# Two z tiles move from the attention's fill to a pair of seven block products between the gates

## The chip, the core and the metric

One Trainium2 chip, one NeuronCore. TensorE (PE) does matmuls and transposes into PSUM, VectorE (DVE), ScalarE (ACT) and GpSimd (POOL) do the elementwise work, and SyncE (SP) issues nearly all DMAs from one queue, in order. The metric is the device time of one execution in microseconds. The kernel before takes 902.21 us, the median of three runs from 901.38 to 902.74.

## The reference, cut to what matters

```python
h = rms_norm(x, g_pre[l], NORM_EPS)
proj = jnp.einsum('bsd,dn->bsn', h, w_in[l])
qa, ka, va, fa, za, qb, kb, vb, zb, gates = jnp.split(proj, SPLIT_POINTS, axis=-1)
...
ya = merge_heads(ya) * jax.nn.silu(za)
...
yb = merge_heads(yb) * jax.nn.silu(zb)
gate_a, gate_b = jnp.split(jax.nn.sigmoid(gates), N_BRANCHES, axis=-1)
merged = (gate_a * jnp.einsum('bsw,wd->bsd', ya, w_branch[l, 0])
          + gate_b * jnp.einsum('bsw,wd->bsd', yb, w_branch[l, 1]))
y = jnp.einsum('bsd,de->bse', merged, w_out[l])
x = x + rms_norm(y, g_post[l], NORM_EPS)
```

Sequence 1024, model width 1024. `za` and `zb` are 512 columns each of the same projection as everything else; together they are eight z tiles of 128 columns, kept transposed (128 columns x 1024 positions, float32). They aren't needed until the two attentions are done and their outputs are multiplied by silu(z).

## The kernel before, in words

Every float32 product is made of three matmuls of a rounded part and its remainder: with left operand `hi + lo` and right operand `h0 + h1`, hi h0, hi h1 and lo h0 (`project`, L328 on). A projected tile takes 2 chunks of 512 positions x 8 blocks of 128 along the model width x 3 = 48 matmuls of 128 x 128 on 128 x 512.

The kernel goes through these stages:

1. Norm, transposition of h into `hT` and the v projections.
2. Attention, eight units `u` in a loop: 0 to 3 are the heads of the differential attention, 4 to 7 pairs of heads of the forgetting attention. A unit is cut into groups of two score rows (L492 and L493: scores; L495: DVE takes the minimum that the softmax needs; L501: ACT's exponential; then a scaling on POOL or ACT). The group before has its probabilities transposed on PE (L522), split into parts on ACT and DVE (L525, L526), and multiplied with v (L546).
3. Between groups, the loop calls functions from a list `fill`: the four projection chunks (q and k) of the unit after, then the z tiles that `ZFILL[u]` names, then the sums of squares that `SFILL[u]` names. The count called after each group goes with the share of the unit's weight that is done. A z tile (`z_tasks`, by `spill_tasks`) loads 512 KB of weights, splits them on POOL and DVE, makes 48 matmuls into two accumulators, copies each out on ACT (L433) and stores it to the scratch tensor `z_d[t]` (L434). `ZFILL` gives z tiles 0, 1, none, 2, 3, 4, 5 and (6, 7) to the units 0 to 7. In unit 7, the last task of the list and the `gl` gate's two chunks are cut into pieces by hand (`LATE`, and the lists at the end of the stage).
4. Gates: 16 gate tiles, d = 0 to 7 and two branches. d = 0 is made plainly; d = 1 to 7 are made as pairs (`gates_pair`): the two branches' tiles of one d are one 256 x 1024 matrix, split in 2 x 2 blocks against `hT` in 2 x 2 blocks, and multiplied by seven block products in the place of eight (`wino`, with the combinations of the left side made in `left_operands` and those of the right side, `t_d`, made in stage 1 and loaded in `h_load`). Each block product is 4 x 3 = 12 matmuls (L818), so that a pair takes 84 where plainly it takes 96. A pair needs four combinations on POOL (L780), seven splits (L767 on ACT, L768 on DVE, for two of them on POOL), one copy on ACT (L821), seven sums on DVE (L811), four sigmoids (L880) and four stores (L881).
5. After each pair the attention outputs that `YORD[d]` names are loaded and multiplied by silu(z) (`y_load`, `y_work`; z is read back at L870). `y_work(t, c)` reads `z_d[(t + 4) % 8]`, so z6 is read at d = 5 and z7 at d = 6.
6. The branch products (L978), the merge and the output projection with its own seven products (L818, tiles `x_o`).

The raw weights of a pair are loaded by `gate_raw` (L902) into the two buffers `wraw`; the two loads of the next pair wait until the four combinations and the splits of the one before have read them.

The order of the instructions on each engine isn't the program's alone: when the kernel is built, a planner with costs of its own draws up each engine's order, with the program's order as priority, and takes later instructions forward where earlier ones would wait. `tc.issue_after(i)` keeps what it encloses behind `i`. The order is fixed then; on the chip, engines wait for each other by semaphores.

Of the kernel before, what the change touches and what calls it, by code (L numbers as in the profile page):

```python
# [16 lines left out]
P = 128  # L17
S = 1024
D = 1024
KT = D // P  # L20
NB = S // P
CH = 512
# [11 lines left out]
GFILL = 5  # L34
LATE = ((), ((0, 0, 3),), ((0, 3, 6),), ((0, 6, 8), (1, 0, 2)), ((1, 2, 5),), ())
TAIL = 2
ZFILL = ((0,), (1,), (), (2,), (3,), (4,), (5,), (6, 7))
BIG = 3.0e38
EPS = 1e-6
SUB_EPS = 1e-5  # L40
# [2 lines left out]
QA, KA_, VA, ZA, QB, KB_, VB, ZB, GT = 0, 512, 1024, 1544, 2056, 2568, 3080, 3592, 4104  # L43
# [7 lines left out]
def tile_hybrid_block(  # L51
# [18 lines left out]
    nc = tc.nc  # L70
# [17 lines left out]
        out=trim, in_=trim, pattern=[[-1, P]], base=0, channel_multiplier=1,  # L88
# [25 lines left out]
    z_d = [dram.tile([P, S], F32, name=f"z_d{t}") for t in range(8)]  # L114
# [196 lines left out]
    def load_w(name, src, hi_act=False, lo_pool=False, pieces=None, behind=(None, None)):  # L311
        raw = wpool.tile([P, KT, P], F32, tag="wraw", name=f"raw_{name}")
        for ks, piece in pieces or [(slice(0, KT), src)]:
            nc.sync.dma_start(raw[:, ks], piece)
        hi = wpool.tile([P, KT, P], F32R, tag="whi", name=f"hi_{name}")
        lo = wpool.tile([P, KT, P], F32R, tag="wlo", name=f"lo_{name}")
        with tc.issue_after(behind[0]) if behind[0] else ExitStack():
            if hi_act:
                nc.scalar.copy(hi, raw)
            else:  # L320
                nc.gpsimd.tensor_scalar(hi, raw, 1.0, 1.0, op0=ALU.mult, op1=ALU.mult)
        with tc.issue_after(behind[1]) if behind[1] else ExitStack():
            eng = nc.gpsimd if lo_pool else nc.vector
            eng.tensor_tensor(lo, raw, hi, op=ALU.subtract)
        return hi, lo

    def w_cols(c0):
        return w[:, c0:c0 + P].rearrange("(k p) n -> p k n", p=P)  # L328

# [10 lines left out]
    with ExitStack() as st:  # L340
# [73 lines left out]
            return T, tasks  # L414

        def z_tasks(t):
            return spill_tasks(f"z{t}", (ZA + t * P) if t < 4 else (ZB + (t - 4) * P), z_d[t])

        def spill_tasks(nm, c0, dst):
            box = {}  # L420

            def mk(c):
                def run(ks=range(KT)):
                    if not box:
                        box[0] = load_w(nm, w_cols(c0))
                    if ks[0] == 0:
                        box["ps"] = pj.tile([P, CH], F32, tag="pj", name=f"p{nm}_{c}")
                    ps = box["ps"]
                    lasts[0] = project(ps, box[0], c, ks)
                    if ks[-1] < KT - 1:  # L430
                        return
                    zs = stg.tile([P, CH], F32, tag="raw", name=f"s{nm}_{c}", bufs=4)
                    nc.scalar.copy(zs, ps)  # L433
                    nc.sync.dma_start(dst[:, c * CH:(c + 1) * CH], zs)  # L434
                return run
            return [mk(0), mk(1)]
# [251 lines left out]
        for u in range(8):  # L688
# [8 lines left out]
            if u + 1 < 8:  # L697
                T, tasks = unit_proj(u + 1)
                fill += tasks
            for t in ZFILL[u]:  # L700
                fill += z_tasks(t)
# [70 lines left out]
    def left_operands(nm, a11, a12, a21, a22):  # L772

        comb = {}

        def combine(name, x, y, op):
            if name not in comb:
                comb[name] = wx.tile([P, 4, P], F32, tag="comb", name=f"{name}_{nm}", bufs=4)
                eng = nc.vector if nm in ("o0", "o1") and name in ("S1", "S2") else nc.gpsimd
                eng.tensor_tensor(comb[name], x, y, op=op)  # L780
            return comb[name]

        def s1():
            return combine("S1", a21, a22, ALU.add)

        def s2():
            return combine("S2", s1(), a11, ALU.subtract)

        def get(m):
            v = {1: lambda: a11, 2: lambda: a12, 4: lambda: a22, 5: s1, 6: s2,  # L790
                 3: lambda: combine("S4", a12, s2(), ALU.subtract),
                 7: lambda: combine("S3", a11, a21, ALU.subtract)}[m]()
            pool, tag = ((wpool, "whi"), (wpool, "wlo"), (wx, "wop"))[opn[0] % 3]
            opn[0] += 1
            t = pool.tile([P, 2, 4, P], F32R, tag=tag, name=f"a{m}_{nm}")
            split(t, v, nc.gpsimd if m in (2, 4) and nm not in ("o2", "o3") else nc.vector)
            return t
        return get
# [68 lines left out]
    def y_work(t, c):  # L867
        ys = yz[t // 2][:, t % 2, c * CH:(c + 1) * CH]
        zs = tmp.tile([P, CH], F32, tag="t", name=f"zs{t}_{c}")
        nc.sync.dma_start(zs, z_d[(t + 4) % 8][:, c * CH:(c + 1) * CH])  # L870
        if t < 4:
            rb = tmp.tile([P, CH], F32, tag="t", name=f"rb{t}_{c}")
            nc.sync.dma_start(rb, rs_d[t:t + 1, c * CH:(c + 1) * CH].to_broadcast([P, CH]))
            nc.vector.scalar_tensor_tensor(ys, ys, gsub, rb, op0=ALU.mult, op1=ALU.mult)
        nc.vector.tensor_tensor(ys, ys, zs, op=ALU.mult)
        nc.scalar.activation(zs, zs, AF.Sigmoid)
        nc.vector.tensor_tensor(ys, ys, zs, op=ALU.mult)

    def gate_out(d, br, c, g, src):
        nc.scalar.activation(g, src, AF.Sigmoid)  # L880
        nc.sync.dma_start(g_d[d][br][:, c * CH:(c + 1) * CH], g)  # L881
# [13 lines left out]

    raws, lastraw = {}, [None]

    def gate_raw(d):
        raws[d] = []
        for br in range(2):  # L900
            r = wpool.tile([P, KT, P], F32, tag="wraw", name=f"raw{d}_{br}")
            lastraw[0] = nc.sync.dma_start(r, w_cols(GT + br * D + d * P)).ins  # L902
            raws[d].append(r)

    def h_load():
# [7 lines left out]
                gate_raw(1)  # L913
            h_ops[m] = [[t[:, k, :] for k in range(4)] for t in ts[m]]

    def gates_pair(d, order):
        raw = raws[d]
        left = left_operands(f"g{d}", raw[0][:, 0:4], raw[0][:, 4:8], raw[1][:, 0:4], raw[1][:, 4:8])
        run_all(wino(f"g{d}", left, h_ops, order,
                     *(lambda t, br=br, c=c: gate_out(d, br, c, t, t)  # L920
                       for br in range(2) for c in range(2))))

    ORD = (1, 6, 5, 7, 2, 3, 4)
    GATE = (1, 2, 4, 6, 5, 7, 3)
# [4 lines left out]
    for d in range(1, KT):  # L929
        if d not in raws:  # L930
            gate_raw(d)
        with tc.issue_after(lastraw[0]):
            for t, c in YORD[d]:
                if c == 0:
                    y_load(t)
        gates_pair(d, (1, 2, 3, 4, 6, 5, 7) if d == 1 else GATE if d < KT - 1 else (7, 5, 6, 4, 1, 2, 3))
        if d == 2:
            for c in range(2):
                g = tmp.tile([P, CH], F32, tag="t", name=f"g0_0_{c}")
                nc.sync.dma_start(g, gl_d[:, c * CH:(c + 1) * CH])  # L940
                gate_out(0, 0, c, g, g)
        for t, c in YORD[d]:
            y_work(t, c)
    tst.close()


# [58 lines left out]
    r = {}  # L1005
# [172 lines left out]
```

## Time and profile before

| | us |
|---|---|
| median of three runs | 902.21 (901.38 to 902.74) |
| the profiled execution | 901.03 |
| its span in the profile | 899.3 |
| first projection of attention (start of k, unit 0) | 108.1 |
| plain gate of d = 0 | 582.2 to 593.2 |
| seven pairs of gates | 593.2 to 727.8 |
| branch products | 727.8 to 814.9 |

The profile is of one execution on the one core, and the granted clock of TensorE was 0.998 in it. Busy times are unions of the intervals of an engine's instructions; the matmuls' ends are modelled and overlap the next one's start, so what a matmul costs is read from the distance of starts.

### The profile page before, as it was taken

To read this page: it belongs to the slowest core of one execution; us is meant where nothing else is said; L and a number is where in the kernel's file an instruction comes from. 1 tells how busy PE (TensorE), PEld (TensorE's weight loads), DVE (VectorE), ACT (ScalarE), POOL (GpSimd) and SP (SyncE) were. 2 spreads that over 40 slices of the span, in tenths; PEclk is the share of its full clock that TensorE was granted. 3 is DMA by queue.
4 is the path that set the end of the run, shared out by engine and by line. 5 is a ranking of instruction groups with operands and counts; after the bars stand their busy time and mean duration, and the time that the engine had idled before them with its cause. 6 is when DMAs were issued, how large, how long until landed. Compare 5 with 4: busy or idle time off the path is not lost.

```text
span 899.3 us, 13795 instructions
## 1 busy us (share of the span) xinstructions
PE 882.4 (98%) x4600; PEld 745.4 (83%) x4600; DVE 581.8 (65%) x1122; ACT 430.4 (48%) x865; POOL 406.0 (45%) x398
## 2 busy tenths in 40 slices
PE   8999999999999999999999999999999999999996
PEld 5999987788888878888888888888888888888885
DVE  6766555767666744456647556627766896648896
ACT  7523224665756653364545646724543362314352
POOL 2134224735646535254344435516534323483961
PEclk9999999999999999999999999999999999999999
DMA  8566656756557763645636430397766598210495
GB/s 303 191 241 249 221 160 166 176 139 170 154 136 188 183 172 80 184 98 133 188 94 158 137 105 26 85 410 243 240 200 203 185 359 299 80 39 1 124 194 173
DMA packets 138185, 154.79 MB, mean 172 GB/s; under 512 B 12145, under 2 KB 98161, under 8 KB 137090
## 3 DMA queue, kind: packets, MB, share of 16 engines
q1 hardware_dynamic: 133744, 151.55, 56.2%
q0 software_dynamic: 4224, 2.10, 2.0%
q8 instruction: 36, 0.59, 0.3%
q14 instruction: 35, 0.29, 0.1%
q10 hardware_dynamic: 146, 0.27, 0.1%
HBM read 86.17 MB, written 38.34 MB: 138 GB/s over the span
## 4 chain that ended last, share of the span: by engine, by line
PE 84%; DMA 4%; DVE 3%; ACT 3%; SPq 2%; issue 2%; POOL 2%; POOLq 0%; DVEq 0%; ACTq 0%
PE x_g L818 15%; PE pb L978 10%; PE pv L214 10%; PE pz L334 9%; PE x_o L818 9%; PE pk L334 7%; PE pq L334 6%; PE ypf L546 4%; PE ptf L522 3%; PE ypd L546 2%; PE Sf L492 2%; PE Sf L493 2%; PE pg L334 1%; SPq L366 1%; PE pgl L334 1%
## 5 line engine op out<-in xcount | busy, mean ns | idle before, releaser
L214 PE MATMUL pv<-wvhi,hT 128*128 128x264 f32 (+2 forms) x384 | 88.1, 323 | 1.0 <-ACT wvhi L160 1.0
L334 PE MATMUL pq<-hT,hi_q 128*128 128x512 f32 x256 | 82.1, 395 | 0.0
L334 PE MATMUL pz<-hT,hi_z 128*128 128x512 f32 x256 | 81.7, 394 | 0.3 <-DVE rotq L368 0.2
L334 PE MATMUL pk<-hT,hi_k 128*128 128x512 f32 x256 | 81.7, 393 | 0.0
L978 PE MATMUL pb<-yT,hi_br 128*128 128x512 f32 x256 | 78.8, 389 | 0.0
L818 PE MATMUL x_g<-T,a_g 128*128 128x512 f32 x336 | 78.0, 391 | 0.0
L818 PE MATMUL x_o<-wo_op,a_o 128*128 128x512 f32 x336 | 77.6, 392 | 0.0
L818 PEld LDWEIGHTS x_o<-wo_op,a_o 128*128 128x128 f32 x336 | 63.0, 188 | 14.4 <-DVE a_o L768 0.5
L818 PEld LDWEIGHTS x_g<-T,a_g 128*128 128x128 f32 x336 | 63.1, 188 | 13.8
L214 PEld LDWEIGHTS pv<-wvhi,hT 128*128 128x128 f32 x384 | 64.1, 190 | 7.2 <-ACT wvhi L160 1.7
L526 DVE TENSOR_TENSOR plf<-ptf,phf 128x512 fp32r<-128x512 f32 (+1 forms) x80 | 50.1, 635 | 25.8 <-ACT phf L525 25.1
L501 ACT ACTIVATE Pd<-Pd,mxd 128x128 f32<-128x128 f32 (+7 forms) x64 | 49.8, 778 | 33.6 <-DVE mxd L495 33.5
L618 POOL TENSOR_TENSOR cb<-cb,trim 128x128 f32<-128x128 f32 x64 | 29.3, 462 | 72.0 <-DVE mxf L495 49.9
L214 PE MATMUL pv<-wvlo,hT 128*128 128x256 f32 (+2 forms) x192 | 61.7, 326 | 0.0
L501 ACT ACTIVATE Pf<-Pf,mxf 128x1024 f32<-128x1024 f32 (+3 forms) x64 | 49.7, 777 | 24.4 <-DVE mxf L495 24.1
L818 PE MATMUL x_g<-hT,a_g 128*128 128x512 f32 x252 | 59.1, 392 | 0.0
L623 POOL TENSOR_SCALAR Pf<-Pf,lf 128x1024 f32<-128x1024 f32 (+3 forms) x64 | 47.9, 753 | 21.9 <-DVE lf L622 18.3
L525 ACT CAST phf<-ptf 128x512 fp32r<-128x512 f32 (+1 forms) x80 | 42.6, 543 | 30.7 <-PE ptf L522 26.5
L978 PEld LDWEIGHTS pb<-yT,hi_br 128*128 128x128 f32 x256 | 48.0, 188 | 10.1
L818 PEld LDWEIGHTS x_g<-hT,a_g 128*128 128x128 f32 x252 | 47.3, 188 | 10.4
L334 PEld LDWEIGHTS pz<-hT,hi_z 128*128 128x128 f32 x256 | 47.3, 188 | 9.4 <-DVE rotq L368 0.5
L334 PEld LDWEIGHTS pq<-hT,hi_q 128*128 128x128 f32 x256 | 47.2, 188 | 8.9
(262 smaller groups left out, 2282.1 us busy)
## 6 DMA issues: line engine op xcount, KB each, us to landing
t_d<-t SPq DMA_DIRECT2D x16, 512.0 KB, 4.1
T<-t_d SPq DMA_DIRECT2D x8, 1024.0 KB, 8.3
raw<-in_w_in_dram SPq DMA_DIRECT2D x14, 512.0 KB, 4.8
vb_d<-vbs SPq DMA_DIRECT2D x8, 512.0 KB
va_d<-vas SPq DMA_DIRECT2D x8, 512.0 KB, 3.3
raw_k<-in_w_in_dram SPq DMA_DIRECT2D x8, 512.0 KB, 4.5
raw_q<-in_w_in_dram SPq DMA_DIRECT2D x8, 512.0 KB, 4.7
V<-vb_d SPq DMA_DIRECT2D x4, 1024.0 KB, 6.3
```

What stands on the lines that cost most here:

```text
L214: nc.tensor.matmul(ps[n], lhsT=hT[hp][k // 4][i // 4][:, k % 4, hs], rhs=wt[k][:, a:b], start=first, stop=(k == KT - 1 and hp == 1))
L334: mm = nc.tensor.matmul(ps, lhsT=a[:, k, :], rhs=hT[h][k // 4][c][:, k % 4, :], start=(k == 0 and a is hi and h == 0), stop=(k == KT - 1 a ...
L492: nc.tensor.matmul(ps, lhsT=A[:, qs], rhs=B[:, a:b], start=True, stop=False)
L501: held[0] = nc.scalar.activation(pr[:, 0:n], pr[:, 0:n], AF.Exp, bias=mx[:, len(pcs) - 1:len(pcs)], scale=-1.0, accum_out=le).ins
L522: lasts[0] = nc.tensor.transpose(pt[:, o * P:(o + 1) * P], rows[2 * g + r][:, j * P:(j + 1) * P], ident).ins
L525: nc.scalar.copy(ph[:, 0:n], pt[:, 0:n])
L526: nc.vector.tensor_tensor(pl[:, 0:n], pt[:, 0:n], ph[:, 0:n], op=ALU.subtract)
L546: lasts[0] = nc.tensor.matmul(o, lhsT=a, rhs=b[:, src], start=(j == 0 and n == 0), stop=(odd == 1 and jj == g and n == len(prods) - 1)).ins
L618: nc.gpsimd.tensor_tensor(diag, diag, trim, op=ALU.add)
L623: held[1] = nc.gpsimd.tensor_scalar(p1[:, 0:n], p1[:, 0:n], l1, 1.0, op0=ALU.mult, op1=ALU.mult).ins
L818: nc.tensor.matmul(x[m], lhsT=a[:, ai, k, :], rhs=right[m][bi][k], start=(k == 0 and n == 0), stop=(k == 3 and n == 2))
L978: nc.tensor.matmul(ps, lhsT=a[:, kk, :], rhs=yT[g][h][:, k % 2, sl], start=(k == 0 and a is hi and h == 0), stop=(k == 3 and a is lo))
```

## The change

z tiles 6 and 7 no longer are fill of attention. `ZFILL` is dealt out anew: units 4 and 6 have no z tile, units 5 and 7 have tiles 3 and (4, 5). After the pair of d = 3 and its y work, `z_pair(6)` loads the weight columns of z6 and z7 in the place of two branches' gate columns, makes the seven products with the same right operands, and stores the four results to `z_d[6]` and `z_d[7]` without a sigmoid. `gate_raw` takes the columns as an argument, and `gates_pair` what is done with each result.

```diff
-ZFILL = ((0,), (1,), (), (2,), (3,), (4,), (5,), (6, 7))
+ZFILL = ((0,), (1,), (), (2,), (), (3,), (), (4, 5))
+ZPAIR = {3: (6,)}
...
+    def z_col(t):
+        return (ZA + t * P) if t < 4 else (ZB + (t - 4) * P)
...
-    def gate_raw(d):
+    def gate_raw(d, cols=None):
         raws[d] = []
         for br in range(2):
             r = wpool.tile([P, KT, P], F32, tag="wraw", name=f"raw{d}_{br}")
-            lastraw[0] = nc.sync.dma_start(r, w_cols(GT + br * D + d * P)).ins
+            c0 = cols[br] if cols else GT + br * D + d * P
+            lastraw[0] = nc.sync.dma_start(r, w_cols(c0)).ins
             raws[d].append(r)
...
-    def gates_pair(d, order):
+    def gates_pair(d, order, out=None):
         raw = raws[d]
+        out = out or (lambda br, c, t: gate_out(d, br, c, t, t))
         left = left_operands(f"g{d}", raw[0][:, 0:4], raw[0][:, 4:8], raw[1][:, 0:4], raw[1][:, 4:8])
         run_all(wino(f"g{d}", left, h_ops, order,
-                     *(lambda t, br=br, c=c: gate_out(d, br, c, t, t)
-                       for br in range(2) for c in range(2))))
+                     *(lambda t, br=br, c=c: out(br, c, t) for br in range(2) for c in range(2))))
+
+    def z_pair(t):
+
+        def out(br, c, v):
+            nc.sync.dma_start(z_d[t + br][:, c * CH:(c + 1) * CH], v)
+
+        gate_raw(f"z{t}", [z_col(t + br) for br in range(2)])
+        gates_pair(f"z{t}", GATE, out)
...
         for t, c in YORD[d]:
             y_work(t, c)
+        for t in ZPAIR.get(d, ()):
+            z_pair(t)
     tst.close()
```

More of the change, by code (lines that the diff above doesn't have):

```diff
@@ L416, in z_tasks @@
         def z_tasks(t):
-            return spill_tasks(f"z{t}", (ZA + t * P) if t < 4 else (ZB + (t - 4) * P), z_d[t])
+            return spill_tasks(f"z{t}", z_col(t), z_d[t])
         def spill_tasks(nm, c0, dst):
```

## The prediction

> **What bounds the kernel now.** I read the page first, its busy times and the waits of the matrix engine, then the chain of work in order of time, then stretches of the attention and of the gates.
>
> ```profile
> span 899.3 us, 13795 instructions
> PE 882.4 (98%) x4600; PEld 745.4 (83%) x4600; DVE 581.8 (65%) x1122; ACT 430.4 (48%) x865; POOL 406.0 (45%) x398
> PE 84%; DMA 4%; DVE 3%; ACT 3%; SPq 2%; issue 2%; POOL 2%; POOLq 0%; DVEq 0%; ACTq 0%
> L334 PE MATMUL pz<-hT,hi_z 128*128 128x512 f32 x256 | 81.7, 394 | 0.3 <-DVE rotq L368 0.2
> L818 PE MATMUL x_g<-hT,a_g 128*128 128x512 f32 x252 | 59.1, 392 | 0.0
> ```
>
> PE is busy 98% of the span and carries 84% of the chain that ended last, so PE work that goes is worth its time, if the rest keeps up. But 392 to 394 ns is the drawn length of one 512-column matmul, and matmuls overlap. What one is worth is its spacing, which the chain in order of time shows (start, length, engine, count):
>
> ```profile
> 315.99 7.79 PE pz L334 x34
> 582.20 10.95 PE pg L334 x48
> 593.15 134.67 PE x_g L818 x588
> ```
>
> 7.79 / 34 = 0.229 us for a z matmul, 10.95 / 48 = 0.228 for a plain gate, 134.67 / 588 = 0.229 for a product of the gates' pairs: the same price in every place. The last row also says that the seven pairs (7 x 84 = 588 matmuls) run without a break.
>
> Next, how full the engines are where work is taken out and where it is put. Columns: stretch, length, busy time of PE, PEld, DVE, ACT and POOL, granted clock, DMA share, GB/s.
>
> ```profile
> 234.00:281.00 47.00, 47.00 (x264) 40.69 (x264) 32.75 (x82) 29.86 (x64) 27.92 (x23) 1.00 0.54 135
> 331.00:389.00 58.00, 57.02 (x316) 48.40 (x315) 28.81 (x78) 30.08 (x61) 27.86 (x32) 1.00 0.51 130
> 446.00:505.00 59.00, 58.71 (x335) 50.59 (x334) 35.37 (x97) 31.50 (x72) 26.25 (x40) 1.00 0.58 154
> 364.00:379.00 15.00, 15.00 (x85) 13.06 (x84) 6.76 (x17) 4.99 (x11) 2.99 (x5) 1.00 0.68 190
> 380.00:389.00 9.00, 8.02 (x56) 6.64 (x55) 7.48 (x24) 7.76 (x18) 5.94 (x10) 1.00 0.53 134
> 441.00:449.00 8.00, 8.00 (x59) 7.42 (x58) 7.88 (x21) 7.00 (x15) 4.79 (x7) 1.00 0.54 144
> 481.00:500.00 19.00, 19.00 (x109) 16.53 (x108) 13.06 (x34) 9.92 (x21) 7.71 (x10) 1.00 0.65 186
> 500.00:508.00 8.00, 7.48 (x48) 6.00 (x47) 5.88 (x16) 7.25 (x15) 4.16 (x5) 1.00 0.50 129
> 651.00:670.00 19.00, 19.00 (x85) 15.60 (x84) 12.02 (x17) 7.77 (x15) 8.89 (x6) 1.00 0.59 182
> ```
>
> The first row is about unit 2, the one attention unit that has no z tile today. The second and third are about units 4 and 6, the two that lose theirs; their z matmuls lie in 364 to 379 and 481 to 500. The rows 380:389, 441:449 and 500:508 are the short stretches that follow the z tiles of units 4, 5 and 6, in which PE has almost nothing but scores, transposes and value products. The last row is one pair of the gates, with PE full and DVE at 12.02 of 19.
>
> **The change, part by part.**
>
> *Removed: 96 matmuls of attention* (two tiles, 2 chunks x 8 k x 3). 96 x 0.229 = 22.0 us of PE. With them go, from attention, two weight splits on POOL and DVE and four copies on ACT:
>
> ```profile
> L321 POOL TENSOR_SCALAR hi_z<-raw_z x8: 1051/1056/1065, 153.1 to 498.3; 128x1024 fp32r<-128x1024 f32 x8
> L324 DVE TENSOR_TENSOR lo_z<-raw_z,hi_z x8: 1212/1226/2042, 154.2 to 499.5; 128x1024 fp32r<-128x1024 f32 x8
> raw_z<-in_w_in_dram SPq DMA_DIRECT2D x8, 512.0 KB, 4.9
> z_d<-sz SPq DMA_DIRECT2D x16, 256.0 KB, 4.3
> ```
>
> POOL 2 x 1.06 and DVE 2 x 1.23 us leave attention; none of it is on the path, so it counts nothing by itself. SP loses two loads of 512 KB and four stores there.
>
> *Added: one pair of seven products*, 7 x 12 = 84 matmuls, 84 x 0.229 = 19.2 us of PE, between the pairs of d = 3 and d = 4. So PE as a whole saves 12 x 0.229 = **2.75 us**. What the pair needs beside PE:
>
> ```profile
> L780 POOL TENSOR_TENSOR S_g<-raw x7: 1284/1290/1298, 579.4 to 697.1; 128x512 f32<-128x512 f32 x7
> L768 POOL TENSOR_TENSOR a_g<-raw,a_g x14: 1290/1526/1779, 585.0 to 714.8; 128x512 fp32r<-128x512 f32 x14
> L768 DVE TENSOR_TENSOR a_g<-S_g,a_g x28: 676/693/1784, 584.5 to 720.7; 128x512 fp32r<-128x512 f32 x28
> L811 DVE TENSOR_TENSOR c_g<-x_g,cu_g x14: 675/685/692, 609.7 to 739.1; 128x512 f32<-128x512 f32 x14
> L767 ACT CAST a_g<-raw x21: 602/617/626, 581.2 to 714.2; 128x512 fp32r<-128x512 f32 x21
> ```
>
> POOL: four combinations and two splits, at most 6 x 1.8 = 10.7 us. DVE: five splits and seven sums, 5 x 0.69 + 7 x 0.69 = 8.3 us. ACT: seven casts and a copy, 8 x 0.62 = 4.9 us, no sigmoid. All of it lies beside 19.2 us of PE and is less than a gate pair with its y work has today (12.02 us of DVE in 19). I cost it at nothing; if that cover were gone, DVE would need 19.2 us, and it has 8.3.
>
> *Moved DMAs.* The pair's two loads take both buffers of the raw weights, behind those of d = 3, and the loads of d = 4 go behind the pair's:
>
> ```profile
> raw<-in_w_in_dram SPq DMA_DIRECT2D x14, 512.0 KB, 4.8
> 630.50 0.38 SPq L902 DMA_DIRECT2D raw<-in_w_in_dram  x1
> 634.01 0.54 SPq L902 DMA_DIRECT2D raw<-in_w_in_dram  x1
> SPq L881 <- ACT cp_g L880: 40.7, 6, 9.9
> ```
>
> Pairs begin every 84 x 0.229 = 19.2 us from 593.2, so the loads issued at 630.5 and 634.0 are for the pair at 650.9: landed 4.8 us later they are 12 us early. The z pair is fed in the same way. SP also gets four stores more, which wait for DVE sums and not for ACT. Today SP stands up to 9.9 us behind one gate store, and no product is late for it; behind the z stores are the y loads and the raw loads of d = 4, which have the same 12 us. Cost 0; at the worst one landing late, 4.8 us. The z rows stored here are read by the y work of d = 5 and d = 6, after a whole pair more.
>
> *Cover taken from attention.* This is the term that the trace doesn't show. Within 364 to 379, z fills 48 x 0.229 = 11.0 of 15 us, so 4 us of attention products are covered; within 481 to 500 it is 8 of 19. These 12 us join the stretches without fill. There PE idles 0.98 of 9, 0 of 8 and 0.52 of 8 us: 1.50 in 25, or 6%. 12 x 6% = 0.7 us. Bounds: from below, nothing, since unit 2 with its projections alone keeps PE at 47.00 of 47 while DVE has 32.75; unit 6 without z would come to the same load, (35.37 - 1.23) / 48 = 71% against 32.75 / 47 = 70%. A little below nothing isn't excluded, since POOL, ACT and the projections' accumulators get freer. From above, DVE's work of the two stretches, worked out under the second rival, 4.1 us. I take 0.7: those stretches are the same products in the same units.
>
> By the Trainium skill, "TensorE: Matmul & The Clock Gate", section "Back-to-back issue gap", a lone warm matmul of 512 columns takes about 216 ns, and a stream of weight load and matmul about 131 ns. By these the saving would be 2.59 or 1.57 us; the trace disagrees with the smaller one and has 229 ns in three places.
>
> *The sum.* 22.0 - 19.2 = 2.75 saved, 0.7 given back: -2.0 us. The profiled execution took 901.03 us, 899.3 of span and 1.7 around it; it goes to 899.0. The median of the runs shown, 902.21, is 1.2 above that execution, and the same difference gives **900.2 us**. The bound of 0.2%, about what a measurement of this kernel can tell from no change, is 1.8 us, so the forecast lies only just beyond it.
>
> **The rivals.**
>
> *The saving is eaten (same).* The cover lost costs 0.95 to 4.55 us in place of 0.7. For it: PE's order is fixed beforehand by a planner with costs of its own, so a score or a transpose whose input is late on the chip holds up what is ordered behind it. Its price at the middle is 2.75: **902.2**. That the seven products save nothing, because the pair waits 2.75 us somewhere, gives the same time; 0 idle among 588 products speaks against it.
>
> *VectorE bounds the ends of units 4 and 6 (slower).* Take the z matmuls out of 481 to 508: PE has 19.00 + 7.48 - 11.0 = 15.5 us left, DVE 13.06 + 5.88 = 18.9. In 364 to 389 (without the microsecond at 379) PE has 15.00 + 8.02 - 11.0 = 12.0 left, DVE 6.76 + 7.48 = 14.2. DVE exceeds PE by 3.4 and 2.2 us, of which PE idles 0.5 and 1.0 already: 2.9 + 1.2 = 4.1 us of new waiting where DVE runs without a gap, the upper bound used above. It runs with gaps: 7.48 of 9 us, 83%, in 380 to 389. At that share DVE's 33.1 us take 39.9, 6.8 more: 4.1 + 6.8 - 2.75 = 8.2 us slower, **910.4**. It decides once the new waiting passes 4.55 us. Against it: this needs the planner to leave the stretches without projections, and matmuls of projections can be drawn into them; unit 2 lives on projections alone, and over all of unit 6 DVE has just 71%.
>
> The Trainium skill, "Perfetto Trace Analysis", section "Optimization Strategy", says that where the busiest engine changes from stage to stage, interleaving the stages can help. That speaks against this change, which takes PE-only work out of a mixed stage and gives it to one where PE alone is full; by that rule the second rival comes in. The trace agrees in part: DVE has 7.88 of 8 us in 441:449, yet PE idles none there.
>
> **How the numbers follow.** Forecast, most of the saving stays (loss under 0.95 us): 0.48. Eaten: 0.40. Slower: 0.12. So faster by over 0.2% 0.48, within 0.40, slower 0.12. The range reaches from 899.0 (no loss, 899.5, and half a microsecond of relief) to 904.0, the edge of the slower case: 0.08 below and 0.12 above are left out. The likeliest case's own range is 899.0 to 900.4.
>
> **What would show it.** PE: 4588 matmuls, with 672 in the pairs, one chain of about 672 x 0.229 = 154 us without a break. Attention from the first projection to the plain gate shorter by 21 to 22 us. Idle PE behind the projections of units 4 and 6 under 2.5 us in all, with DVE or ACT as releaser. Wrong if PE waits at L492, L522 or L546 grow by over 2 us, if the chain of pairs breaks at the z pair or behind it, or if idle comes back in unit 7.

## The result, and the profile after

The changed kernel takes 910.5 us (median of 6 runs, 907.14 to 911.59), the kernel before in the same session 901.8 (6 runs, 899.18 to 902.77). The ratio is 1.0097, with an interval of 1.0074 to 1.012. So the change makes the kernel slower by about 1%, where 0.2% faster was forecast. The profiled execution took 910.36 us.

The line numbers of the changed kernel are 4 higher in the attention and the gates: scores L496, DVE's minimum L499, exponential L505, transposes L526, value products L550. The page of the kernel after, its span, busy times and chain:

```profile
span 908.6 us, 13814 instructions
PE 886.1 (98%) x4588; PEld 745.0 (82%) x4588; DVE 586.0 (64%) x1132; ACT 433.3 (48%) x869; POOL 412.2 (45%) x402
PE 83%; DMA 4%; DVE 4%; ACT 3%; POOL 2%; issue 2%; SPq 2%; POOLq 0%; DVEq 0%; ACTq 0%
```

PE has its 12 matmuls less, and by this page it is as full as before, 98%. Nothing here shows the 9 us. Shares of the whole span hide a loss that lies in a few stretches, and a matmul at half the clock counts as busy for longer.

The chain of the kernel after in order of time (start, length, engine, count) shows the gates, with the z pair as `x_gz`, and one link of attention:

```profile
473.36 5.68 DMA sq<-y_d
...
583.28 57.72 PE x_g L822 x252
641.00 19.22 PE x_gz L822 x84
660.22 76.94 PE x_g L822 x336
```

The pairs run without a break, 57.72 + 19.22 + 76.94 = 153.88 us for 672 matmuls, against 134.67 for 588. So the added pair costs its 19.2 us and nothing more.

Then the length of attention, from the first k projection (`pk`) to the first plain gate matmul (`pg`), by the rows of these two tiles (count, then shortest, mean and longest in ns, then first and last start). Before:

```profile
L334 PE MATMUL pk<-hT,hi_k x256: 387/389/500, 108.1 to 470.7; 128*128 128x512 f32 x128
L334 PE MATMUL pg<-hT,hi_g x32: 389/389/445, 582.0 to 592.5; 128*128 128x512 f32 x32
```

After:

```profile
L338 PE MATMUL pk<-hT,hi_k x256: 387/390/498, 107.6 to 460.7; 128*128 128x512 f32 x128
L338 PE MATMUL pg<-hT,hi_g x32: 388/390/499, 572.1 to 582.7; 128*128 128x512 f32 x32
```

Attention took 582.0 - 108.1 = 473.9 us and takes 572.1 - 107.6 = 464.5. It lost 22.0 us of matmuls and got only 9.4 shorter: **12.6 us went**. (The whole span adds up: attention 9.4 shorter, its start 0.5 earlier, the pair 19.2 longer, and 908.6 - 899.3 = 9.3.) The last k projection, the one that unit 6 makes for unit 7, parts the loss roughly. Up to it 362.6 became 353.1, 9.5 of the first tile's 11.0 us. From it to the plain gate 111.3 became 111.4: of the second tile's 11.0 us nothing is kept. That tile's place was the end of unit 6.

There, the waits of 172 us of the kernel before (370 to 542: engine, tile and line, what was waited for, us in total, times, longest):

```profile
PE ssq L448 <- ACT sq L445: 0.6, 1, 0.6
PE Sf L492 <- DVE mxf L495: 0.3, 1, 0.3
```

and of the 172 us of the kernel after that answer to them (360 to 532):

```profile
PE Sf L496 <- DVE mxf L499: 3.0, 4, 1.8
...
ACT sq L447 <- DMA sq<-y_d: 4.7, 1, 4.7
...
PE ssq L452 <- ACT sq L449: 1.9, 1, 1.9
```

`sq` and `ssq` are the sums of squares, the third kind of fill. `sum_squares` loads half a row block of y (`sq<-y_d`), squares it on ACT (L447), rounds it there (L449), takes the remainder on POOL, and sums over the partitions with two matmuls on PE. The timeline of the kernel after, SP's queue and ACT:

```profile
472.72 0.59 SPq L385 DMA_DIRECT2D TB<-hiq  x1
473.36 1.06 SPq L446 DMA_DIRECT2D sq<-y_d  x2
```

```profile
473.90 0.48 ACT L529 CAST phf<-ptf 128x384 fp32r<-128x384 f32 x1
479.06 0.63 ACT L447 ACTIVATE sq<-sq 128x512 f32<-128x512 f32 x1 [4.68 <-DMA sq<-y_d]
479.60 1.02 ACT L505 ACTIVATE Pf<-Pf,mxf 128x896 f32<-128x896 f32 x1
```

The loads go out behind the stores of the last projection, and ACT reaches the square with nothing left ahead of it. It stands 4.68 us, and the next exponential stands behind it in ACT's order. VectorE in the same stretch:

```profile
473.14 1.22 DVE L325 TENSOR_TENSOR lo_z<-raw_z,hi_z 128x1024 fp32r<-128x1024 f32 x1
474.28 0.68 DVE L383 TENSOR_TENSOR loq<-pq,hiq 128x512 fp32r<-128x512 f32 x1
```

These two splits, of a z weight and of q, stand ahead of the minimum that starts at 475.12. The same step of ACT before the change:

```profile
495.22 1.13 SPq L442 DMA_DIRECT2D sq<-y_d  x2
```

```profile
501.27 0.64 ACT L443 ACTIVATE sq<-sq 128x512 f32<-128x512 f32 x1 [0.63 <-DMA sq<-y_d]
```

From issue to square it was 6.05 us before and is 5.70 now: the load is not slower. What differs is what PE had meanwhile. The stretch of 7 us from the load's issue to the square, before (columns as in the prediction):

```profile
495.00:502.00 7.00, 7.00 (x47) 6.24 (x45) 4.39 (x10) 2.58 (x6) 2.29 (x3) 1.00 0.75 253
```

and after, with the 5 us that follow:

```profile
473.00:480.00 7.00, 3.99 (x13) 1.93 (x12) 5.53 (x15) 2.27 (x6) 3.78 (x5) 0.86 0.95 248
480.00:485.00 5.00, 3.72 (x14) 3.28 (x15) 2.99 (x12) 4.92 (x11) 3.70 (x4) 0.52 0.48 114
```

PE made 47 matmuls in seven microseconds, now 13. In 473 to 485 it is idle for 12.00 - 7.71 = 4.3 us, and the granted clock of 0.86 and 0.52 costs at most 0.14 x 7 + 0.48 x 5 = 3.4 us more. Of the idle time, 1.9 us are PE's wait for ACT's rounding ahead of a sum's matmul, and 2.4 us are two waits for DVE's minimum (1.79 and 0.58). The first of these isn't ACT's doing: DVE had its two splits to do, and the minimum then waited 0.16 us for a POOL step that stood behind another load. So the sums' chain is only one of the things on which PE stood here. What both have in common is that PE has no fill: from the last projection of unit 6, at 471.0, to the first z matmul of unit 7, at 486.5, it has attention products and three matmuls of the sums. Before the change that stretch is 498.2 to 507.9. The z tile of unit 6 stood in the list of fill between the projections and the sums, and it was what PE did while the sums' load, square and rounding went by.

The stall is not the whole loss. PE's idle time in attention grew from 5.7 to 11.8 us, so 6.2 of the 12.6; the rest is PE time counted as busy, of which the fallen clock in 473 to 485 explains at most 3.4.

### The profile page after: what moved, and what is told of

The parts are those of the page before. It is cut to its first block, busy times and chain, and to the rows that moved or that the text cites. A ratio compares the mean times of both kernels' runs of the same rounds, so it can differ in the third digit from the quotient of the medians.

```text
span 908.6 us, 13814 instructions
## 1 busy us (share of the span) xinstructions
PE 886.1 (98%) x4588; PEld 745.0 (82%) x4588; DVE 586.0 (64%) x1132; ACT 433.3 (48%) x869; POOL 412.2 (45%) x402
## 4 chain that ended last, share of the span: by engine, by line
PE 83%; DMA 4%; DVE 4%; ACT 3%; POOL 2%; issue 2%; SPq 2%; POOLq 0%; DVEq 0%; ACTq 0%
PE x_g L822 15%; PE pb L993 10%; PE pv L215 9%; PE x_o L822 9%; PE pz L338 7%; PE pk L338 7%; PE pq L338 6%; PE ypf L550 3%; PE ptf L526 3%; PE ypd L550 2%; PE x_gz L822 2%; PE Sf L496 2%; PE Sf L497 1%; PE pg L338 1%; PE Sd L496 1%
## 5 line engine op out<-in xcount | busy, mean ns | idle before, releaser
L822 PEld LDWEIGHTS x_o<-wo_op,a_o 128*128 128x128 f32 x336 | 63.0, 188 | 14.4 <-DVE a_o L772 0.5
L505 ACT ACTIVATE Pd<-Pd,mxd 128x128 f32<-128x128 f32 (+7 forms) x64 | 49.7, 777 | 32.9 <-DVE mxd L499 32.8
L338 PE MATMUL pz<-hT,hi_z 128*128 128x512 f32 x192 | 61.5, 395 | 0.1
L505 ACT ACTIVATE Pf<-Pf,mxf 128x1024 f32<-128x1024 f32 (+3 forms) x64 | 49.7, 777 | 23.0 <-DVE mxf L499 22.4
L338 PEld LDWEIGHTS pk<-hT,hi_k 128*128 128x128 f32 x256 | 47.2, 188 | 9.0 <-ACT sq L454 0.3
```

Of the source, the lines that this page charges most:

```text
L338: mm = nc.tensor.matmul(ps, lhsT=a[:, k, :], rhs=hT[h][k // 4][c][:, k % 4, :], start=(k == 0 and a is hi and h == 0), stop=(k == KT - 1 a ...
L505: held[0] = nc.scalar.activation(pr[:, 0:n], pr[:, 0:n], AF.Exp, bias=mx[:, len(pcs) - 1:len(pcs)], scale=-1.0, accum_out=le).ins
L822: nc.tensor.matmul(x[m], lhsT=a[:, ai, k, :], rhs=right[m][bi][k], start=(k == 0 and n == 0), stop=(k == 3 and n == 2))
```

## The experiments

The theory at this point: the sums of squares at the end of unit 6 have lost the work that covered them. The rivals: VectorE bounds these stretches (the prediction's second), the load is late because of its place in SP's queue, the planner's order is poor wherever any z is missing, or part of the loss comes from the pair. All ratios are against the kernel before in the same session.

### The sums put elsewhere

**Sums at the ends of units 3 and 5, which keep their z, and the same edit without the change as its control:**

```diff
-SFILL = ((), (), (), (0,), (1,), (2,), (3,), ())
+SFILL = ((), (), (), (0, 1), (), (2, 3), (), ())
```

> The changed kernel, with the sums of squares of tiles 0 and 1 in unit 3 and of 2 and 3 in unit 5 (both of which keep a z tile), so that units 4 and 6 have neither. Theory A (ScalarE stands behind the late load of y_d for the sums, sq<-y_d, 4.7 us at 474 to 479, and PE's idling then costs clock): the stall goes, PE idles under 1 us at the end of unit 6, the granted clock there is 1.00, and the time is 900 to 903 us. Theory B (without z there is too little PE work beside VectorE's and ScalarE's at the ends of units 4 and 6, whatever the sums do): the time stays at 908 to 912 us, with PE waiting for DVE at the scores.

> The kernel before with the same move of the sums of squares, as a control. Both theories: within 0.3% of before, 900 to 904 us. Were it faster by over 2 us, a gain of the run before this one would belong to the sums alone.

With the change it took 912.64 us, 1.0137 (1.0109 to 1.0166); without it 910.92, 1.0115 (1.01 to 1.013). The control missed altogether: moving the sums costs 10 us with all eight z tiles in place. Windows of the first:

```profile
475.00:500.00 25.00, 25.00 (x140) 21.72 (x139) 17.51 (x52) 12.36 (x25) 11.55 (x16) 1.00 0.59 154
335.00:350.00 15.00, 11.96 (x37) 7.19 (x37) 3.88 (x14) 9.53 (x17) 13.01 (x13) 0.77 0.16 47
```

and of the control:

```profile
335.00:350.00 15.00, 12.38 (x42) 7.82 (x41) 3.41 (x13) 8.69 (x17) 14.17 (x13) 0.77 0.08 20
```

The end of unit 6 is healed at full clock. But with two tiles' sums in a row PE stands at the end of unit 3, in both kernels (the kernel before has 15.00 of 15 there). The waits are others than in unit 6: in the first kernel 1.1 us at a sum's matmul, 1.4 for POOL's scaling and 0.5 for DVE's minimum, with POOL busy 13.01 of 15 us, and ACT doesn't wait for the sums' load in that window. By the tile rows, attention is 482.1 us without the change and 464.2 with it: with the sums away from units 4 and 6, 17.9 of the 22.0 us come back, not 9.4.

**Sums each one unit earlier:**

```diff
-SFILL = ((), (), (), (0,), (1,), (2,), (3,), ())
+SFILL = ((), (), (0,), (1,), (2,), (3,), (), ())
```

> The changed kernel with each tile's sums of squares one unit earlier (units 2 to 5 in place of 3 to 6), one tile per unit, so that unit 6 has neither z nor sums. The run with the sums moved had 0.2 us of PE standing at the end of unit 6 where the changed kernel has 7.7, but a new 7.7 us at the end of unit 3, with two tiles' sums in it. Theory A' (the stall at a unit's end is that of sums whose loads come late, and two tiles' sums at once are worse than one): the end of unit 6 stays clean, no clock under 0.9 in attention, 902 to 906 us. Theory B (lost cover): the ends of units 4 and 6 still cost, 907 to 912 us.

915.52 us, 1.018 (1.0163 to 1.0197), a miss. Unit 6 is full; units 2 and 4 now have sums and no z. Unit 2's end, in this kernel:

```profile
270.00:300.00 30.00, 21.57 (x111) 16.78 (x110) 21.03 (x50) 19.70 (x44) 19.45 (x19) 0.83 0.67 175
```

and the same stretch before, without sums there:

```profile
270.00:300.00 30.00, 29.47 (x164) 24.98 (x163) 19.62 (x48) 18.91 (x42) 18.14 (x17) 1.00 0.69 173
```

Unit 2 had no z before either, and PE was full. With one tile's sums, four matmuls, PE is busy for 7.9 us less, and the clock falls to 0.83. So here a unit carries projections without z, and not sums on projections alone. But the trace doesn't show PE behind the sums' chain. The deepest part of the hole, and PE's waits in 270 to 300:

```profile
285.00:290.00 5.00, 1.06 (x4) 0.50 (x4) 2.60 (x6) 3.13 (x9) 4.27 (x5) 0.86 1.02 333
```

```profile
PE ptd L526 <- POOL Pd L599: 6.3, 3, 3.9
```

The longest wait, for POOL's scaling, ends at 290.9. The sums' load goes out only at 289.0, their first square starts at 293.4, and their first matmul at 297.1 waits for nothing. What changed ahead of that is where the projections stand: the last one of this unit's list ends at 269.1, and the next one on PE starts at 300.3, where in the kernel before they are spread over the whole stretch. The list of fill is called by the share of the unit's weight that is done, so the last projection, the fourth entry, is called past 3/7 of the weight in a list of seven and past 3/4 in a list of four. So the sums can cost in two ways: by their own chain, and by taking places in the list, which leaves the end of the unit without projections. How much of the second is the list and how much the planner's order, this run doesn't show.

**Sums ahead of the projections and z in the list of fill:**

```diff
+            for t in SFILL[u]:
+                fill += [lambda t=t, c=c: sum_squares(t, c) for c in range(2)]
+                fill.append(lambda t=t: subln_scales(t))
             if u + 1 < 8:
                 T, tasks = unit_proj(u + 1)
                 fill += tasks
             for t in ZFILL[u]:
                 fill += z_tasks(t)
-            for t in SFILL[u]:
-                fill += [lambda t=t, c=c: sum_squares(t, c) for c in range(2)]
-                fill.append(lambda t=t: subln_scales(t))
```

> The changed kernel with the sums of squares ahead of the projections in each unit's list of fill, so that projections lie between their loads and the end of the unit. Theory A: 900 to 904 us, no wait of ACT for sq<-y_d over 1 us in unit 6. Theory B: 908 to 912 us.

914.97 us, 1.0162 (1.0145 to 1.0179), a miss. The stall goes to the start of unit 3 (275 to 295), where the sums now come straight after the unit that makes their y. As in the run before, it is a stretch without projections, from 272.8 to the first sum's matmul at 294.5, and PE's longest wait there is 4.4 us for POOL's scaling.

**The last projection chunk of units 4 and 6 put behind the sums:**

```diff
+            if u in (4, 6):
+                fill.append(fill.pop(3))
```

> The changed kernel with the sums of squares of units 4 and 6 ahead of the last projection chunk (q, second half) and not behind it: the 24 matmuls of the chunk stand where the z tile stood. Theory A'': the stall of 7.7 us at the end of unit 6 shrinks to under 3 us and the clock stays over 0.9: 903 to 907 us. Rival (the sums stall wherever z isn't in the unit, as they did in front of all projections): 909 to 915 us.

907.63 us, 1.0079 (1.0058 to 1.0101), 2.9 us under the changed kernel, though the intervals overlap. Windows around the end of unit 6:

```profile
462.00:470.00 8.00, 6.32 (x35) 5.05 (x34) 6.04 (x16) 4.13 (x11) 2.75 (x5) 0.86 0.73 168
468.00:488.00 20.00, 19.37 (x103) 15.76 (x103) 13.80 (x45) 15.17 (x30) 12.97 (x18) 0.92 0.53 149
```

468 to 488 has 19.37 of 20 us where the changed kernel has 15.71. The chunk stands on PE from 479.4 on, behind the first half of the sums; a smaller stall stays ahead of it. Over all of attention ACT waits 5.7 us for the sums' loads, as in the changed kernel (5.5), but here only 1.6 of it at the end of unit 6, against 4.7. So this run doesn't tell the cover by the chunk from the shorter wait of ACT.

**The sums' load issued by ACT in place of SP:**

```diff
-            nc.sync.dma_start(sq, y_d[t][:, sl])
+            nc.scalar.dma_start(sq, y_d[t][:, sl])
```

> The changed kernel with the sums' loads of y_d issued by ScalarE's queue and not by SyncE's, where they stand behind the stores of the projections. Theory A' : the load in unit 6 is issued some microseconds earlier, ScalarE's wait for it shrinks from 4.7 to under 2 us, the clock stays at 1.00, and the time falls to 902 to 907 us. If it is the load's duration and not its place in the queue, the time stays at 907 to 912 us.

909.37 us, 1.011 (1.0095 to 1.0126), as the changed kernel. The loads go out at 469.3 and 470.9, in place of 473.4, and ACT's longest wait for them there is 2.7 us, in place of 4.7. The end of unit 6:

```profile
475.00:480.00 5.00, 3.37 (x14) 2.55 (x13) 1.92 (x5) 3.40 (x7) 2.03 (x3) 0.50 0.96 223
```

The stall and the half clock are still there. So the place in SP's queue is not what decides. DVE has 1.92 of 5 us, which speaks against VectorE in this window; in the 5 us before it, where PE waits 1.4 us for DVE, DVE has 4.46.

### z put elsewhere, and the pair by itself

**z in unit 6 again, none in unit 5:**

```diff
-ZFILL = ((0,), (1,), (), (2,), (), (3,), (), (4, 5))
+ZFILL = ((0,), (1,), (), (2,), (), (), (3,), (4, 5))
```

> The changed kernel with z tile 3 in unit 6 and none in units 4 and 5. Theory A: the stall sits where sums follow projections without a z tile between, so it goes from the end of unit 6 (6 us) and comes, in whole or in part, at the end of unit 5: 903 to 910 us, with ACT waiting for sq<-y_d there. Theory B: the loss follows the number of units without z, 908 to 912 us, without that wait.

906.68 us, 1.0068 (1.0052 to 1.0084). 3.8 us come back (the intervals just overlap), the granted clock is 0.998 over the span, as before the change, and attention is 461.1 us. But it isn't the kernel before: units 4 and 5 now have sums and no z, and the loss is spread over their ends.

**The missing z in units 1 and 3, so that units 4 to 6 have theirs:**

```diff
+ZFILL = ((0,), (), (), (), (1,), (2,), (3,), (4, 5))
```

> The changed kernel with units 1 and 3 without a z tile, and one tile each in units 4, 5 and 6: the forgetting units keep their cover, two differential units lose theirs. Unit 2 runs without a z tile at an excess of 0.5 us in the kernel before. Theory A' : units 4 and 6 come back to their old shape; unit 3 has sums and no z and may stall at its end by up to 4 us; 898 to 905 us. Theory B: the loss moves to the units that lost z, 905 to 911 us.

904.54 us, 1.0059 (1.0037 to 1.008), the best with the sums where they were. Unit 3 has a sum and no z, and its end, at 295 to 305, shows a hole and then a fallen clock:

```profile
295.00:300.00 5.00, 2.25 (x14) 1.50 (x13) 3.54 (x6) 2.03 (x6) 2.97 (x4) 1.00 0.79 184
300.00:305.00 5.00, 5.00 (x30) 4.81 (x30) 3.25 (x12) 3.50 (x8) 1.50 (x3) 0.66 0.62 188
```

The sums' first load goes out at 298.4, in the middle of the hole, and their first matmul comes at 305.4. PE's waits there are 0.9 us for POOL and 1.8 for DVE, and it has no projection from 293.6 to 309.9. Attention is 459.4 us.

**The missing z in units 0 and 1, where there are no sums:**

```diff
+ZFILL = ((), (), (), (0,), (1,), (2,), (3,), (4, 5))
```

> The changed kernel with units 0 and 1 without a z tile and one in each of units 3 to 6: no unit has sums without a z tile, as in the kernel before. Theory A' : 898 to 902 us, faster than before, since the pair's 2.75 us stay. Theory B: 904 to 911 us, the loss lying in units 0 and 1.

913.87 us, 1.0169 (1.0147 to 1.019), the most surprising miss: every sum has its z, and the kernel is the slowest of this group. A window of this kernel:

```profile
180.00:210.00 30.00, 25.66 (x136) 21.28 (x136) 20.72 (x51) 19.08 (x43) 13.55 (x14) 0.94 0.54 120
```

and of the kernel before:

```profile
180.00:210.00 30.00, 30.00 (x165) 25.63 (x165) 19.95 (x50) 19.49 (x42) 13.29 (x12) 1.00 0.50 123
```

Three units in a row without z leave PE idle without any sums. The waits of this kernel, and after them those of the changed one, over the whole span:

```profile
PE Sd L496 <- DVE mxd L499: 5.6, 7, 1.5
```

```profile
PE Sd L496 <- DVE mxd L499: 1.0, 2, 0.7
```

PE stands at the scores of the differential heads for DVE's minimum. Attention is 466.8 us: 14.9 of the 22.0 lost. So cover has a price of its own, and the sums are not the whole of the loss.

**Units 3 to 6 with one z chunk each, half a tile:**

```diff
+ZFILL = ((0, 1), (2, 3), (), (4,), (5,), (6,), (7,), (8, 9, 10, 11))
...
-            for t in ZFILL[u]:
-                fill += z_tasks(t)
+            for n in ZFILL[u]:
+                if n % 2 == 0 or n - 1 not in ZFILL[u]:
+                    zt = z_tasks(n // 2)
+                fill.append(zt[n % 2])
```

> The changed kernel with the same two z tiles gone, but in halves: units 3, 4, 5 and 6 each keep one chunk of 24 matmuls (tiles 2 and 3, each chunk with its own load of the weights), units 0 and 1 one tile, unit 7 two. Theory A'' (a unit's cover has a threshold: what lies beside the sums and the unit's last rows must not be nothing): no unit is bare, the loss in attention is under 4 us in place of 12.4, no clock under 0.9, 899 to 903 us. Rival (the loss goes with the amount of cover taken, wherever): 907 to 912 us.

905.52 us, 1.0061 (1.0044 to 1.0078). The clock is 0.999 and no stall stands out, yet attention is 459.3 us: 7.4 of the 22.0 lost, and the time too is above what was expected. PE waits four times at the sums for ACT, 0.5 us at the longest.

**Both: z as in the kernel without z in units 1 and 3, each sum a unit later, that of tile 3 between the z tiles of unit 7:**

```diff
+ZFILL = ((0,), (), (), (), (1,), (2,), (3,), (4, 5))
+SFILL = ((), (), (), (), (0,), (1,), (2,), (3,))
...
+            if u == 7:
+                fill = fill[0:2] + fill[4:7] + fill[2:4]
```

> The run without z in units 1 and 3, with the sums of squares one unit later (units 4 to 7, in unit 7 between its two z tiles), so that no unit has sums without z. Theory A'': the 5.8 us at the end of unit 3, where the sums stood alone, shrink to under 1.5; unit 1 keeps its 2.6; 898.5 to 902 us. Rival (cover alone): 903 to 907 us, as with the sums in unit 3.

908.96 us, 1.0098 (1.0078 to 1.0118), a miss: with z in every unit that has sums, PE still waits once for 2.6 us at a sum, at 350.

**All z tiles in attention as before the change, and the pair beside them:**

```diff
+ZFILL = ((0,), (1,), (), (2,), (3,), (4,), (5,), (6, 7))
```

> The change's second half alone: z tiles 6 and 7 stay in attention, in the old places, and the pair computes them once more between the gates and overwrites them (so 84 matmuls are done for nothing). Theory A'' (the pair costs its 19.2 us and nothing else; all of the loss comes from what attention loses as cover): attention is again 474 us long, the pairs 153.9, and the time is that of before plus 19.2, 918.5 to 921.5 us. Rival (the pair disturbs something before it, by its loads or the planner's new order): attention over 477 us and the time over 922 us.

919.48 us, 1.0217 (1.0191 to 1.0244). The pairs take 153.9 us and attention 471.7. The added pair costs its 19.2 us and disturbs nothing; the whole loss is in attention.

### The sums out of attention

If the sums are the cause, then without any in attention the change should get its 2.75 us. Two ways of putting them into the gates were tried.

**Made at one go after a pair's y work**, `SFILL` empty and `sums_late` a copy of the sums' code:

```diff
+SFILL = ((),) * 8
+SGATE = {1: (0,), 2: (1,), 3: (2,), 4: (3,)}
...
         for t, c in YORD[d]:
             y_work(t, c)
+        for t in SGATE.get(d, ()):
+            sums_late(t)
```

> The changed kernel with the sums of squares taken out of attention and made between the gates' pairs (after d = 1 to 4), where PE is always full; 16 of PE's matmuls move with them. Theory S (the sums make most of the loss): attention's time over its matmuls falls from 29 to under 19 us, no clock under 0.9, 897 to 902 us. Theory C (cover as such): over 24 us stay, 903 to 908 us.

> The kernel before with the sums between the gates' pairs: the control of the run above. Both theories: 898 to 901 us, since the sums' waits in attention are some 2 us there. Theory S: 1 to 3 us slower than the run above, since there the pair's 2.75 us remain; theory C: 3 to 8 us faster than it.

> Sums between the gates' pairs, and units 1 and 3 without z in place of 4 and 6. Theory S: the 5.8 us at the end of unit 3 shrink to under 1.5, unit 1 keeps its 2.6: 897 to 901 us. Theory C: 902 to 907 us.

> Sums between the gates' pairs, and units 3 to 6 with half a z tile each. In the run with halves PE stood at or before sums at the ends of units 3 to 6, some 7 us in all above the kernel before. Theory S: 897 to 901 us. Theory C: 902 to 906 us.

| | us | ratio |
|---|---|---|
| with the change | 957.93 | 1.0641 (1.0619 to 1.0663) |
| without it | 956.71 | 1.0619 (1.0603 to 1.0635) |
| with it, no z in units 1 and 3 | 966.31 | 1.0725 (1.0704 to 1.0746) |
| with it, half tiles in units 3 to 6 | 959.19 | 1.0652 (1.0628 to 1.0677) |

All four miss what was expected of their time: they lose some 55 us in the gates, where PE waits for each sum between the pairs. The waits of the one without the change:

```profile
PE ssq L934 <- ACT sq L931: 43.7, 8, 10.9
```

As kernels they are worthless, but attention is free of sums in them. With the change the end of unit 6 is clean at full clock, in a window of that kernel:

```profile
468.00:488.00 20.00, 20.00 (x112) 17.34 (x111) 13.22 (x39) 11.02 (x22) 9.96 (x15) 1.00 0.67 185
```

Attention is 467.1 us without the change and 450.6 with it: 16.5 kept, 5.5 lost. Of the places for the missing z, the change's own is then no worse than the others (450.6; half tiles 450.9, units 1 and 3 459.5).

The last number goes against the theory. Without z in units 1 and 3, attention is 459.4 us with the sums and 459.5 without any, so 14.4 of the 22.0 are lost against 467.1 with no sum to blame. The hole at 295 to 300 is gone (PE 5.00 of 5), but others have come, one in unit 6, between its projections and its z tile:

```profile
460.00:465.00 5.00, 2.59 (x11) 1.68 (x10) 2.62 (x7) 2.80 (x7) 1.32 (x3) 0.93 0.77 164
```

PE stands there without a projection or z matmul from 455.0 to 463.4, and waits 2.4 us for DVE's minimum. So such a stall needs no sums; why z in these two units is worth so much was not found out.

**Spread over the gates**: the squares are taken from the y tiles that `y_load` brings in anyway, and the sums' matmuls come a whole pair later, so that nothing on PE waits for them:

```diff
+SFILL = ((),) * 8
...
+            for t in {1: (0, 1), 3: (2, 3)}.get(d, ()):
+                y_load(t)
...
+        if 2 <= d < 6:
+            sums_late(d - 2)
+        if d < 5:
+            sums_parts(d - 1)
         for t, c in YORD[d]:
             y_work(t, c)
```

> The kernel before with the sums of squares between the gates' pairs, but their matmuls a whole pair behind their loads and ScalarE steps (and the squares taken of the tiles that the y work has loaded anyway). Attention was 467.1 us in the run without sums and without the change, against 473.9; 16 matmuls come to the gates, 3.7 us. If PE no longer stands between the pairs: 896 to 899 us, faster than before by about 3 us. If the pairs are held up by the four buffers that the sums keep: 902 to 915 us.

> The changed kernel with the same deferred sums. Attention was 450.6 us without sums, 16.5 us less than the kernel of the run above; the pair costs 19.2. So the change by itself, without any sums in attention, is expected to lose 2.7 us: 1.5 to 4 us over the run above, 898 to 902 us. If the cover's loss were only that of the sums, it would be 2 to 3 us below the run above.

| | runs | us | ratio |
|---|---|---|---|
| without the change | 11 | 901.28 (899.52 to 903.36) | 1.0007 (0.9998 to 1.0016) |
| with the change | 11 | 899.98 (898.55 to 901.5) | 0.9988 (0.9979 to 0.9997) |

With the sums deferred, the loss of the change is gone: 9 us slower becomes 0.1% faster than the kernel before (900.88 in 21 runs), while the same move without the change leaves the time as it was. That is the theory's main claim, and for the change's own places of z it holds. It shows that the loss goes with the sums in the lists of attention; it doesn't show by which of the two ways. And 0.1% is less than the 0.2% that counts as a gain here. Two expectations failed. The control was to come out at 896 to 899 us and took 901.28. The change was expected 1.5 to 4 us slower than this control, and it is 1.3 us faster, under the 2 to 3 that the theory of the sums alone would give. The tile rows of the control:

```profile
L334 PE MATMUL pk<-hT,hi_k x256: 387/389/499, 106.9 to 462.7; 128*128 128x512 f32 x128
L334 PE MATMUL pg<-hT,hi_g x32: 388/389/451, 575.1 to 585.6; 128*128 128x512 f32 x32
```

and with the change:

```profile
L338 PE MATMUL pk<-hT,hi_k x256: 387/389/500, 108.1 to 449.7; 128*128 128x512 f32 x128
L338 PE MATMUL pg<-hT,hi_g x32: 389/389/445, 558.5 to 569.0; 128*128 128x512 f32 x32
```

Attention is 468.2 and 450.4 us: 17.8 kept, 4.2 lost. PE's idle time in attention is 5.5 us in the control and 7.0 here, so 1.5 of the 4.2 are idle time. Part of it lies in unit 7, a window of the one with the change:

```profile
490.00:520.00 30.00, 28.06 (x187) 23.68 (x186) 24.73 (x78) 22.00 (x51) 13.83 (x25) 1.00 0.28 77
```

PE has 28.06 of 30 us, where the control has 29.09 in the stretch that lies as far behind its last k projection. PE's waits in this window, 1.8 us in all, are for DVE, and DVE is busy 24.73 of 30.

**The pairs together.** Attention by the same two tile rows, without and with the change:

| sums of squares | without | with | kept of 22.0 | lost |
|---|---|---|---|---|
| at the ends of units 3 to 6 (before, after) | 473.9 | 464.5 | 9.4 | 12.6 |
| at the ends of units 3 and 5 | 482.1 | 464.2 | 17.9 | 4.1 |
| at one go in the gates | 467.1 | 450.6 | 16.5 | 5.5 |
| spread over the gates | 468.2 | 450.4 | 17.8 | 4.2 |

Where no sum stands at the end of a unit that lost its z, the change loses 4.1 to 5.5 us in attention; where one does, 12.6. What goes with the sums is the difference, 7.1 to 8.5 us, by single profiled executions. The 7.7 us at most read from 473 to 485 (4.3 idle, up to 3.4 of clock) are of that size. This is said of z taken from units 4 and 6, not of other places.

**What stays open** is the sign of the change without the sums. By single profiled executions it costs 4.1 to 5.5 us for 2.75 saved, so it should come out 1.4 to 2.8 slower. By the medians it is 1.7 slower, 1.2 slower and 1.3 faster in the three pairs. The profiled execution of the deferred control was its fastest, 899.52 against a median of 901.28, so that pair of traces overstates the cost. All of this is near 0.2%. How much of those 4.1 to 5.5 us comes from the load of the engines and how much from the order that the planner fixes wasn't taken apart either, nor how much of the sums' part is their chain and how much their places in the list.

## Why the prediction was wrong

- **The saving on PE (2.75 us): right.** 4588 matmuls, the pair one chain of 19.22 us, foretold 19.2.
- **The pair's other work and the moved DMAs at nothing: right.** The stretch of the z pair in the kernel after:

```profile
641.00:660.00 19.00, 19.00 (x85) 15.61 (x84) 12.35 (x18) 7.78 (x14) 8.70 (x7) 1.00 0.67 208
```

  PE full, DVE at 12.35 of 19. The kernel with all z tiles twice shows the same by time: 19.2 us and nothing beside it.
- **"Cover taken from attention", 0.7 us with bounds of 0 and 4.1: wrong, and the step that failed.** It measured 12.6. It was asked what z covers, and only scores, transposes and value products were counted. The sums of squares were left out, though `SFILL` places them right behind z in the list, and though `ssq` and `sq` stood in the waits of the kernel before. With them in the lists of the units that lost z, 7.1 to 8.5 us more were lost than without. Their chain (a load of about 6 us, ACT, ACT, PE) had no PE work beside it, and their places in the list leave the unit's end without projections; the runs show both, and not the share of each.
- **Unit 2 as the precedent: wrong.** It keeps PE full without z while its list holds nothing but projections, which then reach to its end; with one tile's sums in the list it has 7.9 us less of PE in 30. A likeness of engine loads (71% and 70% of DVE) said nothing of what stands in the list and in what order.
- **The cover as such: its size was off too.** Where no sums interfere it is 4.1 to 5.5 us for the change's places, not 0.7, and 14.4 for units 1 and 3. An idle share of 6%, read where z stands near, was carried over to 12 us that lost it. 4.1 was the upper bound of that step, and it was close to the truth for this part; it already exceeds the 2.75 saved.
- **The clock was taken as granted at 1.00.** In the stall it fell to 0.52, up to 3.4 us.
- **The second rival gave 910.4, and 910.5 was measured: the closeness is luck, though its reason holds in part.** Of the 4.3 us that PE stood in the stall, 2.4 were waits for DVE's minimum. DVE had 5.53 of 7 us there, not far from the rival's 83%, but then 2.99 of 5. The other 1.9 us were for ACT, which had stood for a load, and the rival had neither the sums nor the clock in it. PE's waits for DVE are larger in the kernel without z in units 0 and 1, 5.6 us at the differential scores.
- **The rule cited beside that rival held in the main.** The Trainium skill, "Perfetto Trace Analysis", "Optimization Strategy", favours interleaving of stages with different limits. The runs agree by the profiled executions: all kernels with two z tiles less in attention lose more there than 2.75 us, the least 4.1. By the medians the pair with deferred sums does not, being 1.3 us faster with the change.
- **The signs named ahead.** Waits at L492, L522 and L546 (now L496, L526, L550) were named as the mark of failure, and L496 did grow, from 0.3 to 3.0 us. The wait at the sums' matmul, 1.9 us, wasn't on the list, and it led to the sums.

## What to carry to other kernels

Before filler work is moved away from an engine that bounds, list everything that the filler stands beside: small chains with a load or an in-order engine in them, and what the rest of the list does when an entry goes or comes. Here the place of a few small sums decided whether the change cost 9 us or nothing. A precedent is one only if it has the same chains and the same list, not the same busy shares. And when a stall turns up, a run with the suspect moved needs the same move without the change as its control: here that move alone cost 10 us.

## What the hardware showed beside this

The granted clock fell by half though PE was never idle for long. PE's timeline in the kernel after, around the fall:

```profile
473.61 0.40 PE L497 MATMUL Sf<-KB,X1f 128*128 128x512 f32 x1
475.80 0.50 PE L496 MATMUL Sf<-KB,TB 128*128 128x512 f32 x1 [1.79 <-DVE mxf L499]
...
478.79 0.63 PE L497 MATMUL Sf<-KA,X0f 128*128 128x512 f32 x1
481.28 0.64 PE L452 MATMUL ssq<-sq,onesr 128*32 128x512 f32 x1 [1.86 <-ACT sq L449]
```

The longest gaps between the records are 1.79 and 1.86 us, yet the clock was 0.86 in 473 to 480, with PE at 3.99 of 7 us, and 0.52 in the 5 us after. The Trainium skill, "TensorE: Matmul & The Clock Gate", "HAM oscillation", has as its rule that PE shouldn't be idle for more than about 3.4 us at a time. Here a stretch of short gaps was enough; what share of idle time decides was not measured.
